# Modulation of a hybrid DiT layer: two of eight weight pieces multiplied whole in fp32, more load buffers, the first latent norms queued behind the modulation's rows

## Chip, core and metric

The kernel runs on one core of one Trainium2 chip. The metric is the device time of one execution in microseconds (us); a smaller number is better. Times before were taken in three runs, and one execution was profiled.

## What is computed

One layer (DEPTH 1) of a diffusion backbone over 2048 latent tokens and 256 context tokens of width 1024, all in float32. It begins with the adaLN modulation, from which everything else takes its input:

```python
def _layer(x, ctx, c, c_ctx, ..., w_mod, b_mod, w_in, ...):
    shift, scale, gate = jnp.split(jax.nn.silu(c) @ w_mod + b_mod, 3, axis=-1)
    shift_c, scale_c, gate_c = jnp.split(jax.nn.silu(c_ctx) @ w_mod + b_mod, 3, axis=-1)
    h = _rmsnorm(x, norm_w) * (1.0 + scale[:, None]) + shift[:, None]
    hc = _rmsnorm(ctx, norm_w) * (1.0 + scale_c) + shift_c
    w_state, w_rest = w_in[:, :N_STATE], w_in[:, N_STATE:]
    ...
```

`w_mod` is 1024 x 3072. The change concerns the first two thirds of it (shift and scale, 1024 x 2048, 8 MB), the two vectors `c` and `c_ctx` that it multiplies, and the order of the first norms. Behind it stand the projections of `h` and `hc` by `w_in`, a bidirectional gated DeltaNet, a windowed attention, their merge and the output projection; the change leaves their code as it is.

## The kernel before

The kernel is written in a tile framework. A scheduler, which works with a model of time of its own, orders the instructions of each engine when the program is built, and the engines then run these queues strictly in order, with semaphores between them. `tc.issue_after(ins)` adds no semaphore: it only makes instructions of the block stand behind `ins` in the queue of the engine on which `ins` runs.

**Splitting.** The TensorE multiplies in `float32r`, one pass at reduced mantissa. To keep fp32 accuracy the kernel splits each operand into a rounded part and the rest: `wmh` is the rounded copy that ScalarE (ACT) writes, `wml` is `wm - wmh`, which VectorE (DVE) writes.

**Modulation (lines 260 to 327).** The rows `c`, `c_ctx`, `norm_w` and `b_mod` are loaded and transposed; `silc` is silu of the two vectors, 128 x 8 x 2, and `sil4` holds its rounded part in columns 0 and 1 and the rest in columns 2 and 3. Then come two halves, `j = 0` (shift) and `j = 1` (scale). Each half goes through eight pieces `k` of `w_mod`, 128 x 1024 (512 KB) each:

- line 303: SyncE (SP) issues the load of the piece into one of seven buffers `wm`
- line 306: ACT rounds it into `wmh`; line 307: DVE writes `wml` (two buffers each)
- line 310: four matmuls of 512 columns add the products of `sil4[:, k]` with both parts into two PSUM tiles `mps` of 4 x 512; the four rows are two vectors by two parts

After the pieces 2 and 3 of the first half the two context blocks are loaded (`load_x`, line 280) and normalized (`norm_x`, lines 289 to 295: a sum of squares half on ACT and half on DVE, a power -0.5 on GpSimd at line 72, one multiplication on DVE).

At the end of a half, line 318 copies the two `mps` into one row tile `mrow`, the first 512 columns on ACT and the others on DVE; `mrow` takes its buffer from those of `wm`. Line 321 turns the rows into columns with eight small fp32 matmuls by `sel`, which also adds the two parts; line 323 adds the bias into `modT`. The first half gives `modB` (line 325), the second `modA` (line 327). `wm_dma` is the last load of a piece; loads that are not to stand ahead of it use `issue_after(wm_dma.ins)`.

**What waits for it.** `make_h` transposes normalized blocks (line 336), applies `modA` and `modB` on ACT (line 337), and splits the result into `hh` (GpSimd, line 339) and `hl` (DVE, line 340). First comes `make_h(pre, ...)` for the two context blocks. `tm_weights` loads the state columns of `w_in` in eight pieces `wr` with three buffers (line 357) and splits them (ACT line 358, DVE line 359). `tm_dense` (lines 366 to 368) multiplies, `state_pair` finishes. The loop `for gi in range(8)` then loads two latent blocks at a time, normalizes them (`norm_x`, line 489), makes their `h` and multiplies. All this is the first stage; the long projections follow.

**Space.** The tiles of the modulation lie in the pool `p0m` at the upper end of the SBUF. When it is closed, the pools `hB2` (`hh3`, `hl3`, 32 KB a partition), `hC` (`hh4`, `hl4`, 16 KB) and `p1a` (among others `wn`, `vst`, `kh`, `ks`, `cw`, some 15 KB) take their place in this order from above, and `p1w` with `wr` lies below them. A tile that overlaps an earlier one waits for the last use of that one alone.

Of the kernel before, what the change touches and what calls it, by code (L numbers as in the profile page):

```python
# [7 lines left out]
F32 = mybir.dt.float32  # L8
F32R = mybir.dt.float32r
# [7 lines left out]
L, LC, D = 2048, 256, 1024  # L17
KT = D // 128
NB, NCB = L // 128, LC // 128
# [9 lines left out]
def f32(ap):  # L29
    return ap.bitcast(F32)  # L30


def hybrid(tc, ins, out, dbg=None, upto=9):
    nc = tc.nc
    V, S, G, T = nc.vector, nc.scalar, nc.gpsimd, nc.tensor
    ctx = ExitStack()
    with ctx:
        _hybrid(ctx, tc, nc, V, S, G, T, ins, out, dbg, upto)


def _hybrid(ctx, tc, nc, V, S, G, T, ins, out, dbg, upto):
# [28 lines left out]
    def rsq(o, x, j=0):  # L70

        G.tensor_tensor(o, x, expo[:, j:j + 1].to_broadcast(list(x.shape)), op=ALU.pow)
# [5 lines left out]
    silc = pers.tile([128, KT, 2], F32, name="silc")  # L78
# [66 lines left out]
    def psum(tag, shape, dt=F32, name=None):  # L145
        _, p, banks = pst["left" if tag in pst["left"][2] else "right"]
        return p.tile(shape, dt, name=name or tag, tag=tag, bufs=banks[tag])
# [104 lines left out]
    if True:  # L252
# [3 lines left out]
        pm = pm_.__enter__()  # L256
# [14 lines left out]
        sil4 = pm.tile([128, KT, 4], F32R, name="sil4")  # L271
        V.tensor_copy(sil4[:, :, 0:2], silc)
        V.tensor_tensor(sil4[:, :, 2:4], silc, f32(sil4[:, :, 0:2]), op=ALU.subtract)
        sel = pm.tile([4, 2], F32, name="sel")
        V.tensor_tensor(sel, ident[0:4, 0:2], ident[0:4, 2:4], op=ALU.add)

        def load_x(c):
            xt = px.tile([128, D], F32, name="xt")
            src = ins["ctx"][0, c * 128:(c + 1) * 128] if c < NCB else ins["x"][0, (c - NCB) * 128:(c - NCB + 1) * 128]
            dma(xt, src)  # L280
            return xt

        def norm_x(c, xt):
            ss = px.tile([128, 2], F32, name="ss")
            for j in range(2):
                junk = px.tile([128, 512], BF16, name="junk", bufs=1)
                xs = xt[:, j * 512:(j + 1) * 512]
                if j == 0:
                    S.activation(junk, xs, AF.Square, scale=D ** -0.5, accum_out=ss[:, j:j + 1])
                else:  # L290
                    junk2 = px.tile([128, 512], BF16, name="junk2", bufs=1)
                    V.scalar_tensor_tensor(junk2, xs, 1.0 / D, xs, op0=ALU.mult, op1=ALU.mult, accum_out=ss[:, j:j + 1])
            V.tensor_scalar(ss[:, 0:1], ss[:, 0:1], ss[:, 1:2], EPS, op0=ALU.add, op1=ALU.add)
            rsq(rstd[:, c:c + 1], ss[:, 0:1])
            V.tensor_scalar(xt, xt, rstd[:, c:c + 1], None, op0=ALU.mult)

        pre = []
        modT = pm.tile([128, 16, 2], F32, name="modT")
        for j in range(2):
            mps = [psum("acc" if n == 0 else "hps", [4, 512], name=f"mps{n}") for n in range(2)]  # L300
            for k in range(KT):
                wm = pm.tile([128, D], F32, name="wm", bufs=7)
                wm_dma = dma(wm, ins["w_mod"][0, k * 128:(k + 1) * 128, j * D:j * D + D])
                wmh = pm.tile([128, D], F32R, name="wmh", bufs=2)
                wml = pm.tile([128, D], F32R, name="wml", bufs=2)
                S.copy(wmh, wm)
                V.tensor_tensor(wml, wm, f32(wmh), op=ALU.subtract)
                for w in (wmh, wml):
                    for n in range(2):
                        T.matmul(mps[n], lhsT=sil4[:, k], rhs=w[:, n * 512:(n + 1) * 512],  # L310
                                 start=k == 0 and w is wmh, stop=k == KT - 1 and w is wml)
                if j == 0 and 2 <= k < 2 + NCB:
                    c = k - 2
                    pre.append(load_x(c))
                    norm_x(c, pre[c])
            mrow = pm.tile([4, D], F32, name="mrow", tag="wm", bufs=7)
            for n in range(2):
                (V.tensor_copy if n % 2 else S.copy)(mrow[:, n * 512:n * 512 + 512], mps[n])
            mtp = psum("kt", [128, 8, 2], name="mtp")
            for i in range(8):  # L320
                T.matmul(mtp[:, i], lhsT=mrow[:, i * 128:i * 128 + 128], rhs=sel, start=True, stop=True)
            mt = modT[:, j * 8:j * 8 + 8]
            V.tensor_tensor(mt, mtp, bm[:, j * 8:j * 8 + 8].unsqueeze(2).to_broadcast([128, 8, 2]), op=ALU.add)
            if j == 0:
                V.tensor_copy(modB, mt)
            else:
                V.scalar_tensor_tensor(modA, mt, 1.0, nw.unsqueeze(2).to_broadcast([128, KT, 2]), op0=ALU.add, op1=ALU.mult)

        def make_h(xts, hi, lo, cc):
            n = len(xts) * 128  # L330
            for k in range(0, KT, 2):
                h32 = px.tile([128, 2, 256], F32, name="h32", bufs=2)
                for i in range(2):
                    ps = psum("hps", [128, 512])
                    for j, xt in enumerate(xts):
                        T.transpose(ps[:, j * 128:(j + 1) * 128], xt[:, (k + i) * 128:(k + i + 1) * 128], ident)
                    S.activation(h32[:, i, :n], ps[:, :n], AF.Identity, scale=modA[:, k + i, cc:cc + 1],
                                 bias=modB[:, k + i, cc:cc + 1])
                G.tensor_scalar(hi[:, k:k + 2], h32[:, :, :n], 1.0, 1.0, op0=ALU.mult, op1=ALU.mult)
                V.tensor_tensor(lo[:, k:k + 2], h32[:, :, :n], f32(hi[:, k:k + 2]), op=ALU.subtract)  # L340
# [21 lines left out]
        def tm_dense(c, wh, wl, n):  # L362
            ps = acc([128, 512], name="tmps")
            xh, xl = hsrc(c)
            for k in range(KT):
                T.matmul(ps[:, :n], lhsT=xh[:, k], rhs=wh[:, k], start=k == 0, stop=False)
                T.matmul(ps[:, :n], lhsT=xl[:, k], rhs=wh[:, k], start=False, stop=False)
                T.matmul(ps[:, :n], lhsT=xh[:, k], rhs=wl[:, k], start=False, stop=k == KT - 1)
            return ps[:, :n]
# [113 lines left out]
        for gi in range(8):  # L483
            xts = []
            for j in range(2):
                c = NCB + gi * 2 + j
                with tc.issue_after(wm_dma.ins):
                    xts.append(load_x(c))
                norm_x(c, xts[j])
            o = gi % 2 * 256  # L490
            make_h(xts, hh[gi // 2][:, :, o:o + 256], hl[gi // 2][:, :, o:o + 256], 0)
            if gi == 7:
                px_.__exit__(None, None, None)
                wq_ = tc.tile_pool(name="wts", bufs=2, reuse_waits="tile")
                wq = wq_.__enter__()
            c = NCB + gi * 2
            state_pair(c, [tm_dense(c + j, wh, wl, NST) for j in range(2)])
# [1088 lines left out]
```

## Time and profile before

| | us |
|---|---|
| median of three runs | 2004.95 |
| lowest and highest of them | 2003.56 and 2009.0 |
| span of the profiled execution | 2004.9 |

| engine | busy us in the span | share |
|---|---|---|
| TensorE, matmul (PE) | 1921.2 | 96% |
| VectorE (DVE) | 1509.2 | 75% |
| ScalarE (ACT) | 807.4 | 40% |
| GpSimd (POOL) | 692.6 | 35% |

The profile has one page and a trace behind it that answers further views: groups of instructions by line, waits, a timeline, and windows. In the timeline a row gives the start, the duration, the engine, the line, the operation, what it writes and reads, how many instructions are merged in it, and in brackets the idle time of the engine before it and what ended that. SPq is the queue of DMA issues: its rows are the times of the issue, not of the data. In the windows a row gives a stretch of the span, the busy time and number of instructions of each engine, the granted TensorE clock (1.00 is full speed), the busy share of the 16 DMA engines and the GB/s that they moved. Busy time of PE counts a matmul from its start to a modelled end, so that matmuls that follow each other overlap.

### The profile page before, as it was taken

Reading aid. Unit: us, or ns where it says so; the run is one execution under the profiler, and the core shown is the slowest. Engines: PE = TensorE matmul, PEld = TensorE weight load, DVE = VectorE, ACT = ScalarE, POOL = GpSimd, SP = SyncE. Lnnn points to the kernel's source line nnn. Section 1 sums busy time; section 2 is a strip of 40 time slices with the busy share of each in tenths; the row PEclk is TensorE's granted clock in tenths of the full one; section 3 lists DMA queues with packets and bytes.
Section 4 is the critical chain, followed back from the end, with each engine's and each line's share of the span. In section 5 each row is a group of like instructions: output and inputs, shape, how many; then the busy total and the mean of one; then the engine's idle time right before and its main releaser. Section 6 shows DMA issues by size and latency. Waiting matters only on the chain. (4 is left out here: it accounts for less than half of the span.)

```text
span 2004.9 us, 32107 instructions
## 1 busy us (share of the span) xinstructions
PE 1921.2 (96%) x10947; PEld 1611.0 (80%) x10947; DVE 1509.2 (75%) x2871; ACT 807.4 (40%) x1998; POOL 692.6 (35%) x768
## 2 busy tenths in 40 slices
PE   6999999989999999999999999999989999999998
PEld 3888888779998778877888888788768888877786
DVE  6979766667776899999777776535587777747888
ACT  5755545554444322111222233224675655532221
POOL 1652210225543202004222233323456444420675
PEclk8999999999999999999999999999999999999999
DMA  7542326764546733537887777755355555456454
GB/s 252 175 127 94 98 87 154 184 162 157 161 143 166 189 113 113 142 90 216 225 255 221 224 213 217 193 176 165 126 187 173 176 162 165 129 165 211 137 169 136
DMA packets 387704, 333.12 MB, mean 166 GB/s; under 512 B 83993, under 2 KB 307537, under 8 KB 386901
## 3 DMA queue, kind: packets, MB, share of 16 engines
q1 hardware_dynamic: 352244, 288.60, 49.9%
q10 hardware_dynamic: 35296, 42.48, 6.0%
q8 instruction: 87, 1.43, 0.3%
q14 instruction: 77, 0.62, 0.1%
HBM read 220.28 MB, written 109.13 MB: 164 GB/s over the span
## 5 line engine op out<-in xcount | busy, mean ns | idle before, releaser
L524 PE MATMUL rps<-hh,wh 128*128 128x512 f32 x768 | 309.6, 403 | 5.0 <-DVE rt L818 3.8
L526 PE MATMUL rps<-hh,wl 128*128 128x512 f32 x768 | 309.0, 403 | 0.0
L525 PE MATMUL rps<-hl,wh 128*128 128x512 f32 x768 | 307.7, 401 | 0.0
L563 DVE SCALAR_TENSOR_TENSOR cacc<-y,cw,cacc 128x512 f32<-128x512 f32 (+1 forms) x224 | 163.2, 750 | 22.9 <-ACT cacc L561 18.9
L524 PEld LDWEIGHTS rps<-hh,wh 128*128 128x128 f32 x768 | 145.7, 190 | 39.8 <-DVE rt L818 4.3
L525 PEld LDWEIGHTS rps<-hl,wh 128*128 128x128 f32 x768 | 145.8, 190 | 32.7
L526 PEld LDWEIGHTS rps<-hh,wl 128*128 128x128 f32 x768 | 145.7, 190 | 32.8
L524 PE MATMUL lps<-hh,wh 128*128 128x512 f32 (+1 forms) x448 | 171.6, 383 | 0.2 <-ACT y L634 0.2
L525 PE MATMUL lps<-hl,wh 128*128 128x512 f32 (+1 forms) x448 | 171.3, 382 | 0.0
L526 PE MATMUL lps<-hh,wl 128*128 128x512 f32 (+1 forms) x448 | 171.2, 382 | 0.0
L945 DVE TENSOR_TENSOR pl<-pt,ph 128x512 fp32r<-128x512 f32 x156 | 105.4, 685 | 41.9 <-ACT ph L943 41.2
L943 ACT CAST ph<-pt 128x512 fp32r<-128x512 f32 x156 | 90.2, 585 | 109.9 <-PE pt L941 76.8
L917 DVE CUSTOM_DVE_ANT_0 pr<-sc,band,sk 128x640 f32<-128x640 f32 (+1 forms) x128 | 106.6, 862 | 34.4 <-PE sc L913 18.3
L816 ACT ACTIVATE rt<-rps 128x512 f32<-128x512 f32 x96 | 57.3, 596 | 181.6 <-PE rps L526 167.8
L749 DVE TENSOR_TENSOR N<-N,btmp 128x62 f32<-128x62 f32 (+30 forms) x124 | 117.2, 945 | 3.0
L747 DVE TENSOR_TENSOR btmp<-N 128x62 f32<-128x62 f32 (+30 forms) x124 | 116.6, 940 | 3.1
L927 POOL TENSOR_SCALAR pr<-pr,sm 128x640 f32<-128x640 f32 (+1 forms) x128 | 99.7, 799 | 55.5 <-DVE sm L925 39.0
L919 ACT ACTIVATE pr<-pr,sm 128x640 f32<-128x640 f32 (+1 forms) x128 | 104.0, 815 | 20.4 <-DVE sm L917 20.4
L246 DVE TENSOR_TENSOR wl<-wr,wh 128x512 fp32r<-128x512 f32 x120 | 92.7, 786 | 24.7 <-POOL wh L245 21.9
L1231 PE MATMUL pps<-yh,wph 128*128 128x512 f32 x256 | 104.8, 411 | 4.3 <-ACT yh L1211 2.2
L245 POOL TENSOR_SCALAR wh<-wr 128x512 fp32r<-128x512 f32 x72 | 48.6, 690 | 170.3 <-PE lps L525 97.2
L1232 PE MATMUL pps<-yl,wph 128*128 128x512 f32 x256 | 100.9, 396 | 0.0
(374 smaller groups left out, 5044.2 us busy)
## 6 DMA issues: line engine op xcount, KB each, us to landing
wr<-in_w_in_dram SPq DMA_DIRECT2D x120, 256.0 KB
kw<-Ksp SPq DMA_DIRECT2D x28, 384.0 KB
x<-vsp SPq DMA_DIRECT2D x36, 256.0 KB
k<-ksp SPq DMA_DIRECT2D x34, 256.0 KB
kT<-kTsp SPq DMA_DIRECT2D x34, 256.0 KB
wm<-in_w_mod_dram SPq DMA_DIRECT2D x16, 512.0 KB
xt<-in_x_dram SPq DMA_DIRECT2D x16, 512.0 KB
dtl<-Dsp SPq DMA_DIRECT2D x32, 256.0 KB
```

The source lines that it names most:

```text
L524: T.matmul(ps, lhsT=wh[:, k], rhs=xh[:, k], start=k == 0, stop=False)
L525: T.matmul(ps, lhsT=wh[:, k], rhs=xl[:, k], start=False, stop=False)
L526: T.matmul(ps, lhsT=wl[:, k], rhs=xh[:, k], start=False, stop=k == kt - 1)
L563: V.scalar_tensor_tensor(a, y[:, t:t + n], cw[:, m, t:t + 1], a, op0=ALU.mult, op1=ALU.add)
L747: V.tensor_tensor(tv, A[:, m + 1:, m].unsqueeze(2).to_broadcast([h1 + n, r, m]), A[:, m, 0:m].unsqueeze(1).to_broadcast([h1 + n, r, m]), o ...
L749: V.tensor_tensor(A[:, m + 1:, 0:m], A[:, m + 1:, 0:m], tv, op=ALU.add)
L917: V.tensor_tensor_reduce(s_, ps[:, o:768], band[:, b0:b0 + W + 256], -0.125, sk[:, 1, hd:hd + 1], ALU.add, ALU.min, sm[:, h, 1:2])
L919: S.activation(s_, s_, AF.Exp, scale=-1.0, bias=sm[:, h, 1:2], accum_out=sm[:, h, 2:3])
L927: G.tensor_scalar(p[:, h, :W + 256], p[:, h, :W + 256], sm[:, h, 3:4], 1.0, op0=ALU.mult, op1=ALU.mult)
L945: V.tensor_tensor(pl, pt, f32(ph), op=ALU.subtract)
L1231: T.matmul(ps, lhsT=wh[:, k, ms], rhs=hs[k], start=k == 0, stop=False)
L1232: T.matmul(ps, lhsT=wh[:, k, ms], rhs=ls[k], start=False, stop=False)
```

## The change

Pieces 3 and 7 of each half are no longer split: they are multiplied as they came, in fp32, by `silz`, which holds `silc` in columns 0 and 1 and zeros in 2 and 3, so that the sum still has four rows. Each of their two matmuls is one `T.matmul` call. The load buffers `wm` (and with them `mrow`) go from seven to nine, `wmh` and `wml` from two to three each. The context blocks are loaded and normalized behind the pieces 4 and 6 in place of 2 and 3. The instructions of `norm_x` for the first two latent blocks (`gi == 0`) stand behind the two copies of the second half's rows (line 318) on ACT and on DVE; their loads are not bound so.

```diff
+        silz = pm.tile([128, KT, 4], F32, name="silz")
+        V.memset(silz, 0.0)
+        V.tensor_copy(silz[:, :, 0:2], silc)
...
+        WHOLE = (3, 7)
...
-                wm = pm.tile([128, D], F32, name="wm", bufs=7)
+                wm = pm.tile([128, D], F32, name="wm", bufs=9)
                 wm_dma = dma(wm, ins["w_mod"][0, k * 128:(k + 1) * 128, j * D:j * D + D])
-                wmh = pm.tile([128, D], F32R, name="wmh", bufs=2)
-                wml = pm.tile([128, D], F32R, name="wml", bufs=2)
+                if k in WHOLE:
+                    for n in range(2):
+                        T.matmul(mps[n], lhsT=silz[:, k], rhs=wm[:, n * 512:(n + 1) * 512], start=False, stop=k == KT - 1)
+                    continue
+                wmh = pm.tile([128, D], F32R, name="wmh", bufs=3)
+                wml = pm.tile([128, D], F32R, name="wml", bufs=3)
...
-                                 start=k == 0 and w is wmh, stop=k == KT - 1 and w is wml)
-                if j == 0 and 2 <= k < 2 + NCB:
-                    c = k - 2
+                                 start=k == 0 and w is wmh, stop=False)
+                if j == 0 and k in (4, 6):
+                    c = k // 2 - 2
                     pre.append(load_x(c))
                     norm_x(c, pre[c])
-            mrow = pm.tile([4, D], F32, name="mrow", tag="wm", bufs=7)
-            for n in range(2):
-                (V.tensor_copy if n % 2 else S.copy)(mrow[:, n * 512:n * 512 + 512], mps[n])
+            mrow = pm.tile([4, D], F32, name="mrow", tag="wm", bufs=9)
+            rows_out = [(V.tensor_copy if n % 2 else S.copy)(mrow[:, n * 512:n * 512 + 512], mps[n]) for n in range(2)]
...
-                norm_x(c, xts[j])
+                with ExitStack() as behind:
+                    if gi == 0:
+                        for r in rows_out:
+                            behind.enter_context(tc.issue_after(r.ins))
+                    norm_x(c, xts[j])
```

## The prediction

> **What bounds the kernel now.** I began with the page. PE is busy in 96% of the span, so time is won only where the PE row is thin, and that is its first digit. The change lies there too.
>
> ```profile
> span 2004.9 us, 32107 instructions
> PE   6999999989999999999999999999989999999998
> ```
>
> The windows show what each engine does there:
>
> ```profile
> 10.00:20.00 10.00, 6.32 (x20) 1.63 (x19) 8.48 (x14) 6.37 (x10) 2.07 (x2) 0.98 1.03 410
> 20.00:30.00 10.00, 9.57 (x40) 4.66 (x39) 6.30 (x8) 4.66 (x6) 0.00 (x0) 0.68 0.77 261
> 26.00:27.00 1.00, 1.00 (x7) 0.86 (x6) 0.96 (x3) 0.00 (x0) 0.00 (x0) 0.71 0.13 12
> 43.00:44.00 1.00, 0.51 (x2) 0.11 (x2) 1.00 (x4) 0.35 (x2) 1.00 (x2) 0.50 0.00 0
> 80.00:90.00 10.00, 8.68 (x69) 8.06 (x69) 9.89 (x29) 8.76 (x26) 7.28 (x9) 1.00 0.67 222
> 180.00:220.00 40.00, 40.00 (x198) 33.07 (x197) 34.41 (x61) 23.90 (x56) 10.00 (x9) 1.00 0.32 96
> ```
>
> From 180 us PE is full (40.00 of 40). Before that, while the latent blocks are made, DVE is nearly full (9.89 of 10) and PE close behind (8.68). Neither has a fixed start: if the work before them ends earlier by some time, they end earlier by it. So the question is when the modulation ends. The loads ran at 410 GB/s at first and at 12 GB/s at 26 us. SP's own waits tell why: its loads stood waiting for buffers, for `wml` to have read them or for the first `mrow` to be done with.
>
> ```profile
> SPq L303 <- DVE wml L307: 12.6, 8, 3.1
> SPq L303 <- PE mtp L321: 3.7, 1, 3.7
> ```
>
> The timeline gives the end of the modulation:
>
> ```profile
> 36.54 0.63 PE L310 MATMUL mps<-wml,sil 128*4 128x512 f32 x2
> 36.97 0.57 ACT L318 COPY mrow<-mps 4x512 f32<-4x512 f32 x1 [0.68 <-PE mps L310]
> 39.68 0.69 DVE L292 SCALAR_TENSOR_TENSOR junk<-xt 128x512 bf16<-128x512 f32 x1 [2.06 <-DMA xt<-in_x_dram]
> 40.30 0.67 DVE L318 COPY mrow<-mps 4x512 f32<-4x512 f32 x1
> 40.30 0.08 DVE L292 DVE_READ_ACCUMULATOR junk<-xt 128x1 f32 x1
> 41.81 0.21 DVE L293 TENSOR_SCALAR ss<-ss 128x1 f32<-128x1 f32 x1
> 41.03 1.86 PE L321 MATMUL mtp<-sel,mrow 4*128 4x2 f32 x8 [2.38 <-DVE mrow L318]
> 43.70 0.16 DVE L327 SCALAR_TENSOR_TENSOR modA<-modT,craw 128x16 f32<-128x16 f32 x1
> 43.90 1.94 ACT L337 ACTIVATE h<-hps,modB,modA 128x256 f32<-128x256 f32 x4 [0.65 <-DVE modA L327]
> ```
>
> The last product ends at 37.17 us (36.54 + 0.63). ACT copies its half at once. DVE's half is copied only at 40.30, although it was ready: in DVE's queue a norm stands ahead of it, and that waited for the load of a latent block until 39.68. The columns, `modA` and the first `h` at 43.90 all follow from this copy.
>
> **The rows behind the norms.** With the norms behind both copies, DVE copies right after the last product. Alone this takes 40.30 back to about 37.3, since DVE was idle then: **3.0 us**. What the norm's edge holds back on DVE and ACT is only the norms. Two of them cost DVE 2 x (0.69 + 0.08 + 0.21) = 2.0 us and fit beside the 1.86 us of line 321, for which DVE waits anyway; if they ran ahead of `modT` and late, they would cost up to 1 us. Their loads are not held.
>
> **Two pieces whole.** The rows for a split piece and for an fp32 matmul:
>
> ```profile
> L307 DVE TENSOR_TENSOR wml<-wm,wmh 128x1024 fp32r<-128x1024 f32 x16 | 19.3, 1223 | 2.9 <-ACT wmh L306 2.6
> L306 ACT CAST wmh<-wm 128x1024 fp32r<-128x1024 f32 x16 | 16.7, 1048 | 8.7 <-DMA wm<-in_w_mod_dram 3.1 <-DVE wml L307 2.0 <-PE hps L336 1.7
> 7.64 1.01 PE L310 MATMUL mps<-wmh,sil 128*4 128x512 f32 x2 [3.33 <-ACT wmh L306]
> 30.41 0.62 PE L310 MATMUL mps<-wml,sil 128*4 128x512 f32 x2
> 30.87 0.61 PE L310 MATMUL mps<-wmh,sil 128*4 128x512 f32 x2
> 21.06 1.05 PE L310 MATMUL mps<-wml,sil 128*4 128x512 f32 x2
> 21.92 1.05 PE L310 MATMUL mps<-wmh,sil 128*4 128x512 f32 x2
> 745.92 1.02 PE L227 MATMUL gsum<-gacc,mats 128*1 128x512 f32 x2
> 746.87 0.50 PE L524 MATMUL rps<-hh,wh 128*128 128x512 f32 x1
> ```
>
> Four pieces fewer on DVE are 4 x 1.22 = 4.9 us and on ACT 4 x 1.05 = 4.2 us. On PE a pair of split products takes 0.46 us (30.41 to 30.87) at full clock and 0.86 (21.06 to 21.92) at half: 0.93 or 1.71 a piece. The kernel has one fp32 matmul of 512 columns, line 227; it is recorded as two instructions, and the next product follows after 0.95 us. Its stationary side has one column and not four, which should not matter, since the split products have four. A whole piece thus costs 2 x 0.95 = 1.9 us, or by the ratio of the clocks an estimated 3.8 at half clock. PE pays 1 us more for each of the four.
>
> **More buffers.** A load of 512 KB at 410 GB/s takes 1.28 us. The first piece is there by 6.55:
>
> ```profile
> 6.55 1.04 ACT L306 CAST wmh<-wm 128x1024 fp32r<-128x1024 f32 x1 [1.75 <-DMA wm<-in_w_mod_dram]
> ```
>
> With nine buffers `mrow` has one of its own, and the last load needs one that piece 7 frees near 20 us. So I take the 18 loads (16 pieces, two context blocks) as unbroken. Piece 7 is the tenth: 6.55 + 9 x 1.28 = 18.1 us. The last: 6.55 + 17 x 1.28 = 28.3.
>
> **The new end of the modulation.** First half: piece 7 lands at 18.1, and its 1.9 us on PE follow directly, where a split piece would pass ACT and DVE first: 20.0. Here the rows stand of the passage between the halves, and the transposes that PE does in it:
>
> ```profile
> 23.55 0.68 DVE L318 COPY mrow<-mps 4x512 f32<-4x512 f32 x1 [1.75 <-PE mps L310]
> 23.94 1.94 PE L321 MATMUL mtp<-sel,mrow 4*128 4x2 f32 x16 [0.43 <-ACT mrow L318]
> 26.28 1.34 PE L336 MATMUL hps<-ident,xt 128*128 128x128 f32 x6
> ```
>
> Second half: copy 0.7, line 321 1.94, transposes 1.34, then 6 x 0.93 + 2 x 1.9 = 9.4 us of products. By then DVE (six pieces of 1.22 since 20 us) and the loads (28.3) are ahead, so PE is the limit: 20.0 + 0.7 + 1.9 + 1.3 + 9.4 = 33.3 at full clock. The granted clock was 0.68 in the mean from 20 to 30 us; if it was full or half, that is 6.4 us at half, and half of these falling into the second half's products would add 1.6: 34.9. Where the transposes or first products fill PE while it waits for the copy, up to 1.5 us go off. Bounds 32 to 36; I take **34.0**, between. The Trainium skill, "TensorE: Matmul & The Clock Gate", Part 1, speaks against the change: an idle TensorE falls to half rate and comes back only after about 3.4 us of sustained work. The passage between the halves would be such an idle time; by the rule the products behind it would end at 35.0 and the kernel at 1999.7, where by the 34.0 above it is 1998.7. The 0.68 agrees with stretches of this kind.
>
> **The sum.** DVE's copy moves from 40.30 to 34.05, 6.25 us. Line 321, the bias and `modA` follow as before, and so does `h`: 43.90 becomes 37.65. To keep it, the state weights must come earlier too:
>
> ```profile
> 27.84 1.37 SPq L357 DMA_DIRECT2D wr<-in_w_in_dram  x3
> 30.68 2.40 SPq L280 DMA_DIRECT2D xt<-in_x_dram  x2
> 36.86 8.37 SPq L357 DMA_DIRECT2D wr<-in_w_in_dram  x5
> 42.12 1.13 ACT L358 CAST wh<-wr 128x272 fp32r<-128x272 f32 x3 [0.39 <-DMA wr<-in_w_in_dram]
> L358 ACT CAST wh<-wr x8: 410/417/418, 35.1 to 47.0; 128x272 fp32r<-128x272 f32 x8
> L337 ACT ACTIVATE h<-hps,modB,modA x72: 548/567/623, 43.9 to 132.3; 128x256 f32<-128x256 f32 x72
> 36.40 1.14 DVE L359 TENSOR_TENSOR wl<-wr,wh 128x272 fp32r<-128x272 f32 x3
> L303 SPq DMA_DIRECT2D wm<-in_w_mod_dram x16: 328/328/646, 2.7 to 27.5; - x16
> ```
>
> They are issued in three and five, with the latent blocks between; the second lot waits until DVE has split the first, from 36.40 on. All stand behind the last piece's load, which leaves SP at some 21 (piece 7's buffer comes free at 20.0) in place of 27.5 us, and DVE has its last `wml` near 30 (the second half's piece 6 lands at 6.55 + 16 x 1.28 = 27.0, then 1.05 + 1.22) in place of 36.4. So they come some 6 us earlier. The last of them was cast at 47.0, 3.1 us behind the first `h`, and eight parts of `h` take ACT 8 x 0.567 = 4.5 us, so this chain had about 1.4 us in hand. `silz` is two small instructions on DVE before the first piece has landed at 6.55; uncovered they would cost about 0.4 us, twice the 0.21 of line 293. The context loads two and three pieces later delay norms whose result PE needs only for transposes: nothing, or the 1 us that is in the bounds. Forecast: 2004.9 - 6.25 = **1998.7 us**. The profiled span and the median of the runs, 2004.95, are the same.
>
> **The rivals.**
>
> *PE takes the place of DVE (slower).* If PE stays at half clock, a half costs 6 x 1.71 + 2 x 3.8 = 17.9 us. In the second half alone: 20.0 + 0.7 + 1.9 + 1.3 + 17.9 = 41.8, the copy then in place of 40.30: 2006.4. In both halves (7.64, where the first product starts, + 17.9 = 25.5): 47.3, 2011.9. It decides from an end of the products at 40.3 us on. For it: 0.50 at 43 us and 0.68 from 20 to 30. Against it: from 10 to 20, with PE busy 6.32 of 10, the clock was 0.98, and the change makes PE busier. 5%, at 2006 to 2012.
>
> *The gain stops at the next load (half of it).* The loads may come later than I let them, by the scheduler's order or because `p0m` grows from 45 to 61 KB a partition and now reaches under `p1a`: the rope tile `cw` then waits for a buffer of `wm`, and SP holds what stands behind it, the second lot of `wr` among it. Then only what the copy gives is kept: 2004.9 - 3.0 = 2001.9. If `cw` waits for the second `mrow`, freed near 37.6, this lot is issued 1 us later than before and nothing is left: 2005. For it: SP waited 3.7 us behind line 321 already. Against it: `cw` can take its turn later, and the chain had 1.4 us in hand. 30% in all: 22% at 2000.5 to 2004, 8% at 2004 to 2006.
>
> *More than forecast.* If PE keeps full clock and fills the gap behind the copy, the products end at 32: 8.2 us, 1996.7; and the stage behind it, at 0.50 where it starts, would win up to 2 us if its half clock ended sooner: 1994.7. 15%.
>
> **How the numbers follow.** The forecast has 50%, from 1996.9 to 2000.5 (ends at 32.2 to 35.8). The range goes from 1995.5 to 2003.5, which leaves out about a tenth on each side. Faster by over 0.3%, about what can be told from no change here, means below 1998.9: somewhat over half of the forecast's 50% and nearly all of the 15%, 0.43; slower by over 0.3% (above 2011) needs the first rival in both halves or a stage behind that is reordered badly, 0.06; the rest, 0.51, lies within.
>
> **What would show it.** In the profile of the changed kernel: DVE's copy of the second rows within 0.2 us of the last product, and that product at 32 to 36 us; records of fp32 matmuls on the whole pieces 0.47 us apart, two for a matmul; no wait of SP's line 303 for line 321; the first `h` near 37.7; the second lot of `wr` cast by 40; and from the first `h` to the end 1961.0 us as before (2004.9 - 43.9). It is wrong if the products end above 37, if `h` waits for PE, SP or `wr` instead, or if those 1961.0 us have another length, which nothing here foresees.

## The result, and the profile after

| | before | after |
|---|---|---|
| median of 20 executions, us | 2002.93 | 1998.24 |
| lowest and highest, us | 1995.94, 2009.0 | 1992.38, 2003.26 |
| span of the profiled execution, us | 2004.9 | 2001.3 |
| ratio after / before, 95% interval | | 0.9976 (0.9967 to 0.9985) |

The changed kernel is faster by 0.24%, that is 4.8 us of 2002.93 (3.0 to 6.6). The forecast was a gain of 6.25 us and 1998.7 us. That 1998.7 and the measured 1998.24 lie so close is in part luck: the forecast took its gain off 2004.9, and the kernel before came out at 2002.93 in twenty executions.

DVE's part of the timeline of the changed kernel, around the modulation's second half:

```profile
21.16 0.68 DVE L325 COPY mrow<-mps 4x512 f32<-4x512 f32 x1 [0.16 <-PE mps L310]
23.03 0.17 DVE L330 TENSOR_TENSOR modT<-mtp,craw 128x16 f32<-128x16 f32 x1 [1.19 <-PE mtp L328]
...
23.32 6.90 DVE L315 TENSOR_TENSOR wml<-wm,wmh 128x1024 fp32r<-128x1024 f32 x6
...
34.03 0.68 DVE L325 COPY mrow<-mps 4x512 f32<-4x512 f32 x1 [2.67 <-PE mps L310]
...
36.16 0.17 DVE L330 TENSOR_TENSOR modT<-mtp,craw 128x16 f32<-128x16 f32 x1
36.24 0.43 DVE L366 TENSOR_TENSOR wl<-wr,wh 128x272 fp32r<-128x272 f32 x1
36.67 0.75 DVE L298 TENSOR_SCALAR xt<-xt,rstd 128x1024 f32<-128x1024 f32 x1
37.34 0.21 DVE L296 TENSOR_SCALAR ss<-ss 128x1 f32<-128x1 f32 x1
37.47 0.17 DVE L334 SCALAR_TENSOR_TENSOR modA<-modT,craw 128x16 f32<-128x16 f32 x1
```

The second copy of the rows starts at 34.03, released by the product that ended at 33.99 (the row of PE below, 32.11 + 1.88). DVE sat idle for 2.67 us before it, so nothing stands in its way. Before, it started at 40.30, 3.1 us after the last product. From `modT` at 36.16 to `modA` at 37.47, however, DVE splits a piece of `wr`, scales a normalized block and does a small step of the next norm, none of which `modA` needs: 1.3 us.

PE from the end of the first half on:

```profile
17.55 0.62 PE L318 MATMUL mps<-wml,sil 128*4 128x512 f32 x2 [0.96 <-DVE wml L315]
...
19.24 1.88 PE L310 MATMUL mps<-wm,silz 128*4 128x512 f32 x4
...
27.43 1.88 PE L310 MATMUL mps<-wm,silz 128*4 128x512 f32 x4
29.24 0.63 PE L318 MATMUL mps<-wmh,sil 128*4 128x512 f32 x2
29.70 0.62 PE L318 MATMUL mps<-wml,sil 128*4 128x512 f32 x2
...
32.11 1.88 PE L310 MATMUL mps<-wm,silz 128*4 128x512 f32 x4
33.92 1.94 PE L328 MATMUL mtp<-sel,mrow 4*128 4x2 f32 x16
```

A whole piece is four records and 1.88 us; a pair of split products stands 0.46 us from the next. ACT's rows and the issues of SP behind it:

```profile
37.67 1.93 ACT L344 ACTIVATE h<-hps,modB,modA 128x256 f32<-128x256 f32 x4 [1.60 <-DVE modA L334]
39.48 0.43 ACT L365 CAST wh<-wr 128x272 fp32r<-128x272 f32 x1
40.67 0.42 ACT L365 CAST wh<-wr 128x272 fp32r<-128x272 f32 x1 [0.76 <-DMA wr<-in_w_in_dram]
```

```profile
37.08 0.42 SPq L388 DMA_DIRECT2D wn<-in_k_norm_w_dram  x1
38.01 0.33 SPq L364 DMA_DIRECT2D wr<-in_w_in_dram  x1
```

The first `h` is at 37.67 and was at 43.90. The last piece of `wr` is issued only at 38.01, behind the small load `wn`, and ACT idles 0.76 us until it has landed.

Three marks of each profile serve below: the end of the modulation's products, the first `h`, and the first long projection (first start of `lps` in the views by tile), which ends the latent stage.

### The profile page after: what moved, and what is told of

Same layout as the page of the kernel before. It is cut to its first block, busy times and chain, and to the rows that moved or that the text cites. A ratio compares the mean times of both kernels' runs of the same rounds, so it can differ in the third digit from the quotient of the medians.

```text
span 2001.3 us, 32092 instructions
## 1 busy us (share of the span) xinstructions
PE 1919.3 (96%) x10947; PEld 1606.1 (80%) x10947; DVE 1508.1 (75%) x2869; ACT 802.4 (40%) x1994; POOL 692.2 (35%) x768
## 5 line engine op out<-in xcount | busy, mean ns | idle before, releaser
L956 DVE TENSOR_TENSOR pl<-pt,ph 128x512 fp32r<-128x512 f32 x156 | 105.4, 686 | 41.9 <-ACT ph L954 41.2
```

Source lines behind the costliest of these rows:

```text
L956: V.tensor_tensor(pl, pt, f32(ph), op=ALU.subtract)
```

## The experiments

Edits are against the changed kernel where nothing else is said. Ratios are to the kernel before, run on the same chip; the kernels themselves stood on several chips. Each rests on 10 to 20 executions of the kernel named, but for "after, again" (4) and "the same, 7 load buffers" (5). "Order" says whether PE, DVE, ACT, POOL and SP issue the same instructions in the same order behind the modulation as the changed kernel does; the kernel before does, but for a few at the start. Stage is from the first `h` to the first `lps`. Marks and spans are of the one profiled execution.

| kernel | ratio (95%) | products end | first `h` | first `lps` | stage | span | order |
|---|---|---|---|---|---|---|---|
| before | 1 | 37.2 | 43.9 | 138.7 | 94.8 | 2004.9 | same |
| before, again | | 36.4 | 41.9 | 137.2 | 95.3 | 2007.0 | same |
| after | 0.9976 (0.9967 to 0.9985) | 34.0 | 37.7 | 134.4 | 96.7 | 2001.3 | same |
| after, again | 0.9957 (0.9940 to 0.9974) | 35.3 | 39.0 | 133.6 | 94.6 | 1994.5 | same |
| rows first alone | 1.0009 (0.9996 to 1.0021) | 35.3 | 42.0 | 137.0 | 95.0 | 2004.5 | other |
| without rows first | 1.0003 (0.9984 to 1.0021) | 34.7 | 38.3 | 141.4 | 103.1 | 2005.4 | other |
| all pieces split | 1.0035 (1.0019 to 1.0052) | 38.0 | 44.5 | 142.2 | 97.7 | 2014.0 | other |
| all split, context late | 1.0004 (0.9988 to 1.0021) | 34.8 | 41.2 | 136.5 | 95.3 | 2006.8 | other |
| piece 7 alone whole | 0.9972 (0.9955 to 0.9989) | 34.0 | 37.6 | 133.9 | 96.3 | 1994.3 | same |
| the same, 7 load buffers | 0.9949 (0.9931 to 0.9966) | 34.0 | 37.7 | 134.0 | 96.3 | 1997.5 | same |
| 7 and 2 buffers | 0.9990 (0.9973 to 1.0007) | 34.8 | 38.8 | 133.9 | 95.1 | 2002.6 | other |
| first columns held | 0.9967 (0.9953 to 0.9981) | 34.1 | 37.7 | 133.1 | 95.4 | 1993.3 | same |
| and norms behind `modA` | 0.9975 (0.9962 to 0.9989) | 32.9 | 35.5 | 129.5 | 94.0 | 1996.4 | other |
| `wr` with five buffers | 0.9994 (0.9974 to 1.0013) | 34.1 | 37.8 | 132.3 | 94.5 | 1996.1 | other |

No kernel here is the one before with piece 7 whole and nothing else, and the move of the context blocks was not tried alone.

**The rows first, alone.** The kernel before with this part only:

```diff
-            for n in range(2):
-                (V.tensor_copy if n % 2 else S.copy)(mrow[:, n * 512:n * 512 + 512], mps[n])
+            rows_out = [(V.tensor_copy if n % 2 else S.copy)(mrow[:, n * 512:n * 512 + 512], mps[n]) for n in range(2)]
...
-                norm_x(c, xts[j])
+                with ExitStack() as behind:
+                    if gi == 0:
+                        for r in rows_out:
+                            behind.enter_context(tc.issue_after(r.ins))
+                    norm_x(c, xts[j])
```

> The kernel before with one part of the change alone: the norms of the first two latent blocks stand behind the two copies of the second half's rows. Seven and two buffers, all pieces split, context blocks behind pieces 2 and 3. Theory A (the copy on DVE was held by a norm that waited for a load, and what is behind follows the first h one to one): the last product stays at 37.2 us, DVE copies at about 37.3 in place of 40.3, first h at 40.9, and the time falls by 3.0 us, 0.15%. Rival (the gain of the change comes from loads and pieces; the copy only hid a wait for something else, such as the state weights or the latent block): first h within 1 us of 43.9, time unchanged.

Measured 1.0009: no gain. DVE in its timeline:

```profile
35.69 0.67 DVE L317 COPY mrow<-mps 4x512 f32<-4x512 f32 x1
38.84 0.69 DVE L292 SCALAR_TENSOR_TENSOR junk<-xt 128x512 bf16<-128x512 f32 x1 [2.48 <-DMA xt<-in_x_dram]
...
40.12 0.69 DVE L292 SCALAR_TENSOR_TENSOR junk<-xt 128x512 bf16<-128x512 f32 x1 [0.26 <-DMA xt<-in_x_dram]
...
40.73 0.17 DVE L322 TENSOR_TENSOR modT<-mtp,craw 128x16 f32<-128x16 f32 x1
```

The copy comes at once, at 35.69. But the two norms now stand behind it and still ahead of `modT`, and they wait for the same loads, issued about as late (29.59 us, before 30.68). The wait moved one place down the queue: `modT` comes at 40.73 and the first `h` at 42.0, between the 41.9 and 43.9 of the kernel before.

**Everything but the rows first.**

```diff
-                with ExitStack() as behind:
-                    if gi == 0:
-                        for r in rows_out:
-                            behind.enter_context(tc.issue_after(r.ins))
-                    norm_x(c, xts[j])
+                norm_x(c, xts[j])
```

> The changed kernel without this one part: whole pieces and more buffers stay, the norms of the first two latent blocks are free again. Theory A taken strictly: a norm stands ahead of DVE's copy again, which then waits for the latent block; first h at 40 to 41 us, 3 us later than the 37.7 of the changed kernel. Rival (the latent blocks are now loaded some 5 us earlier, so a norm in front finds its data and runs in the time in which DVE waits for the products anyway): products end at 34.0 as in the changed kernel, DVE copies within 0.5 us of it, and first h is at 36.4 to 37.7, no later and perhaps earlier, because modA no longer stands behind norms.

Its DVE rows:

```profile
31.96 0.68 DVE L295 SCALAR_TENSOR_TENSOR junk<-xt 128x512 bf16<-128x512 f32 x1
...
34.70 0.68 DVE L325 COPY mrow<-mps 4x512 f32<-4x512 f32 x1 [2.05 <-PE mps L310]
```

The norm stands ahead of the copy again, but finds its block at 31.96, since the blocks are now issued from 26.35 us on. The copy waits for PE alone, and the first `h` is at 38.3, 3.6 us behind the last product; with the norms behind it was 3.7. In the head this part is worth nothing beside the others. And yet no gain is left that can be told from noise: 1.0003 (0.9984 to 1.0021). The stage that follows took 103.1 us in the one profile of this kernel, and the windows show DVE emptier in it and PE as busy with fewer matmuls at a lower clock (the second fence is of the changed kernel):

```profile
78.00:98.00 20.00, 17.23 (x104) 16.22 (x105) 15.88 (x43) 11.77 (x31) 12.24 (x15) 0.74 0.42 125
```

```profile
78.00:98.00 20.00, 17.21 (x133) 15.62 (x131) 19.46 (x49) 13.23 (x38) 13.45 (x17) 1.00 0.52 172
```

In the same 20 us PE does 104 matmuls in place of 133 and DVE 43 operations in place of 49. In the program, what differs there is the order alone: without the edge some 60 of PE's and 50 of DVE's instructions of this stage stand elsewhere. So a single part taken out changes two things, the head and the order behind it. The experiments marked "same" are free of this. That the other order is what makes the stage long isn't shown: the kernel with five `wr` buffers and the one with 7 and 2 buffers have about as many instructions elsewhere, and their stages are 94.5 and 95.1 us. Whether the lower clock follows from the order or came by itself, one profile doesn't say.

**All pieces split.**

```diff
-        WHOLE = (3, 7)
+        WHOLE = ()
...
-                                 start=k == 0 and w is wmh, stop=False)
+                                 start=k == 0 and w is wmh, stop=k == KT - 1 and w is wml)
```

> The changed kernel with no whole piece: all eight are split in each half, nine and three buffers, norms behind the rows. Theory A (with DVE's share of two pieces back, DVE and not PE limits the second half, but only by a little): products end at 34.5 to 35.5 us in place of 34.0, first h 38.2 to 39.2, whole pieces worth about 1 us. Rival (the 4.9 us that they take off DVE count in full for the second half's part, 2.4 us and more): products end at 36.4 or later, first h at 40 or later.

PE around the end of its first half, and the windows of the same execution:

```profile
19.43 0.63 PE L318 MATMUL mps<-wmh,sil 128*4 128x512 f32 x2
22.42 0.78 PE L318 MATMUL mps<-wml,sil 128*4 128x512 f32 x2 [2.37 <-DVE wml L315]
23.48 3.57 PE L328 MATMUL mtp<-sel,mrow 4*128 4x2 f32 x16 [0.28 <-ACT mrow L325]
```

```profile
20.00:22.00 2.00, 0.05 (x1) 0.00 (x0) 1.52 (x2) 0.00 (x0) 0.45 (x1) 1.00 1.05 420
22.00:24.00 2.00, 1.30 (x5) 0.61 (x5) 1.04 (x2) 1.15 (x2) 0.00 (x0) 0.68 1.00 399
24.00:26.00 2.00, 2.00 (x11) 2.00 (x11) 0.00 (x0) 2.00 (x3) 0.00 (x0) 0.50 1.05 418
...
30.00:32.00 2.00, 2.00 (x6) 0.55 (x5) 2.00 (x2) 0.99 (x1) 0.00 (x0) 0.50 0.70 281
```

The last piece must pass ACT and DVE, where a context norm stands ahead of it, and PE waits 2.37 us for it. Behind this pause the granted clock is 0.50 until about 32 us, and line 328 takes 3.57 us and not 1.94. The products end at 38.0, the first `h` is at 44.5, and the kernel is slower than before: 1.0035. The order behind differs too, so how much of the time the head alone costs isn't known.

**All split, the context blocks behind the pieces 6 and 7**, so that no norm stands ahead of the last piece's split:

```diff
-        WHOLE = (3, 7)
+        WHOLE = ()
...
-                if j == 0 and k in (4, 6):
-                    c = k // 2 - 2
+                if j == 0 and k in (6, 7):
+                    c = (6, 7).index(k)
```

> No whole piece, nine and three buffers, norms behind the rows, and the context blocks behind the pieces 6 and 7; the order behind the modulation differs in some 60 places on TensorE and 70 on VectorE. Theory A (the whole last piece is what saves PE from waiting for ACT and DVE at the end of each half, where a wait can cost the full clock): products end at 35 to 38.5 us, first h at 39 to 44; the time is then 1.5 to 6 us above the changed kernel. Rival (what made the kernel without whole pieces slow was only the order of the stages behind it): products end at 34 to 35, and the time is within 1.5 us of the changed kernel.

The products end at 34.8, nearly as early as with whole pieces, though at half clock from 21 to 27 us:

```profile
21.00:27.00 6.00, 5.68 (x26) 4.99 (x25) 4.62 (x8) 4.23 (x5) 0.56 (x1) 0.50 1.02 409
```

The first half ends where it does in the changed kernel: DVE copies its rows at 21.15 and there at 21.16. So in these two profiles the end of the products owes only 0.8 us to the whole pieces, once no norm stands ahead of the last split; this end fits the rival. But `modA` comes only at 40.24 and the first `h` at 41.2. DVE has its last `wml` at 34.1 in place of 30.2, its splits of `wr` come later by as much, SP issues the second lot of `wr` from 34.49 on (30.60 in the changed kernel), and `modT` and `modA` stand among the splits that wait for it; ACT even casts the last piece, at 40.90, ahead of the first `h`. That mark fits theory A. The ratio is 1.0004.

**Piece 7 alone whole.**

```diff
-        WHOLE = (3, 7)
+        WHOLE = (7,)
```

> The changed kernel with only the last piece of each half whole; piece 3 is split. The order of the instructions is that of the changed kernel on every engine, but for the piece itself, so that the stages behind can be compared. Theory A (at full clock the second half is shared between DVE and PE): 1.15 us more on DVE, 1 us less on PE in each half; products end 0 to 1.2 us later than the 34.0 of the changed kernel, first h at 37.7 to 38.9, time 0 to 1.2 us longer. Rival (splitting lets PE idle so long that its clock falls to half, as with no whole piece, where the products ended at 38.1): products end at 36 or later, first h at 40 or later, time 2 us and more longer.

Same order, same end. The rows of DVE and of PE:

```profile
23.42 8.03 DVE L315 TENSOR_TENSOR wml<-wm,wmh 128x1024 fp32r<-128x1024 f32 x7
...
33.99 0.68 DVE L325 COPY mrow<-mps 4x512 f32<-4x512 f32 x1 [1.40 <-PE mps L310]
```

```profile
32.07 1.88 PE L310 MATMUL mps<-wm,silz 128*4 128x512 f32 x4
```

DVE has one more `wml` (8.03 us for seven in place of 6.90 for six) and PE 1 us less; they cancel. The copy is at 33.99 in place of 34.03 and the first `h` at 37.6 in place of 37.7. In the head, piece 3 whole is worth nothing.

**The same with seven load buffers in place of nine** (three of `wmh` and `wml` stay):

```diff
-        WHOLE = (3, 7)
+        WHOLE = (7,)
...
-                wm = pm.tile([128, D], F32, name="wm", bufs=9)
+                wm = pm.tile([128, D], F32, name="wm", bufs=7)
...
-            mrow = pm.tile([4, D], F32, name="mrow", tag="wm", bufs=9)
+            mrow = pm.tile([4, D], F32, name="mrow", tag="wm", bufs=7)
```

> The changed kernel with seven load buffers in place of nine, three each for the split parts; the same order of instructions on every engine. Theory A (unbroken loads move the second half): SP's loads wait for buffers again, the last piece's load leaves SP some 3 to 6 us later than the 21.1 us of the changed kernel, products end 0.5 to 2 us later than 34.0, first h at 38.2 to 39.7. Rival (PE is the limit and the loads have that much in hand): products end within 0.3 us of 34.0, first h within 0.5 of 37.7, the same time.

SP's waits in it, and those of the changed kernel in the second fence:

```profile
SPq L307 <- DVE wml L315: 6.6, 5, 2.1
SPq L307 <- PE mps L310: 5.3, 2, 3.2
```

```profile
SPq L307 <- PE mps L310: 4.3, 2, 2.3
SPq L307 <- DVE wml L315: 2.2, 2, 1.5
```

SP waits 11.9 us for these buffers in place of 6.5, and the modulation ends where it did (34.0 and 37.7). The loads had that much in hand, and two of the nine buffers are worth nothing in the head. The ratio, 0.9949, is the lowest of all, but the changed kernel on the same chip gave 0.9957.

**Seven and two buffers**, the sizes of before, with both pieces whole:

```diff
-                wm = pm.tile([128, D], F32, name="wm", bufs=9)
+                wm = pm.tile([128, D], F32, name="wm", bufs=7)
...
-                wmh = pm.tile([128, D], F32R, name="wmh", bufs=3)
-                wml = pm.tile([128, D], F32R, name="wml", bufs=3)
+                wmh = pm.tile([128, D], F32R, name="wmh", bufs=2)
+                wml = pm.tile([128, D], F32R, name="wml", bufs=2)
```

> The changed kernel with the seven and two buffers of before: whole pieces and the norms behind the rows stay. Theory A (the buffers keep the loads unbroken, which is what moves the second half): SP's loads wait for the first half's mrow again, products end at 35.5 to 37, first h at 39 to 40.5. Rival (the whole pieces alone free the engines, and the loads were early enough): products end at 34.0 to 34.5, first h at 37.7 to 38.2.

The products end 0.8 us later (34.8) and the first `h` 1.1 us (38.8). The first row is ACT's last `wmh`, the second DVE's last `wml`:

```profile
30.02 1.05 ACT L314 CAST wmh<-wm 128x1024 fp32r<-128x1024 f32 x1 [1.96 <-PE mps L318]
31.10 1.23 DVE L315 TENSOR_TENSOR wml<-wm,wmh 128x1024 fp32r<-128x1024 f32 x1 [1.78 <-ACT wmh L314]
```

ACT's last cast waits for PE to be done with an earlier `wmh`; with three of them it ran at 27.03, when its load had landed. So the third buffer for the split parts counts here, not the loads. The ratio is 0.9990, with another order behind; how much of it comes from the head and how much from the order isn't known.

**Two tries to do better.** In the changed kernel DVE stands idle for 1.19 us before `modT` of the first half, and the second half's `wml` wait behind it. The first kernel (piece 7 alone whole) puts `modT` and `modB` of the first half behind the second half's second `wml`; the next also holds DVE's part of the norms until `modA`.

```diff
-        WHOLE = (3, 7)
+        WHOLE = (7,)
...
-                V.tensor_tensor(wml, wm, f32(wmh), op=ALU.subtract)
+                wml_out = V.tensor_tensor(wml, wm, f32(wmh), op=ALU.subtract)
+                if (j, k) == (1, 1):
+                    with tc.issue_after(wml_out.ins):
+                        V.tensor_tensor(held[0], held[1], bm[:, 0:8].unsqueeze(2).to_broadcast([128, 8, 2]), op=ALU.add)
+                        V.tensor_copy(modB, held[0])
...
+            if j == 0:
+                held = (mt, mtp)
+                continue
             V.tensor_tensor(mt, mtp, bm[:, j * 8:j * 8 + 8].unsqueeze(2).to_broadcast([128, 8, 2]), op=ALU.add)
-            if j == 0:
-                V.tensor_copy(modB, mt)
-            else:
+            if j == 1:
```

> The changed kernel with only piece 7 whole and with the first half's bias (modT, modB) behind the second half's first two wml on DVE; the order of all instructions behind the modulation is that of the changed kernel. Theory A (in the second half DVE stood idle for 1.2 us before the bias, and with one whole piece DVE sets the pace): DVE begins the second half's wml at 21.9 in place of 23.3 us, products end at 32.2 to 33.2 in place of 34.0, first h at 36 to 37, time 0.5 to 1.5 us below the changed kernel. Rival (PE, with its rows turned first until 23, is the limit): products end within 0.3 us of 34.0.

```diff
-                V.scalar_tensor_tensor(modA, mt, 1.0, nw.unsqueeze(2).to_broadcast([128, KT, 2]), op0=ALU.add, op1=ALU.mult)
+                modA_out = V.scalar_tensor_tensor(modA, mt, 1.0, nw.unsqueeze(2).to_broadcast([128, KT, 2]), op0=ALU.add, op1=ALU.mult)
...
-                        for r in rows_out:
+                        for r in (rows_out[0], modA_out):
```

> The kernel one_held with the norms of the first two latent blocks behind modA on DVE, in place of behind DVE's copy. In the changed kernel 1.3 us of other work lies between modT and modA. Theory A: first h another 0.9 us earlier than in one_held. The order of the latent blocks' stage differs here from the changed kernel's in some places (about 50 on TensorE, 45 on VectorE). Theory A (a head that is earlier moves all): time 1 us below one_held. Rival (the order of that stage weighs more than the head): the stage from the first h to the first long projection, 94.6 to 96.7 us in the changed kernel, is longer by 2 us and more, and the time is not below one_held's.

The second half became shorter, as meant: from the first copy to the end of the products 22.54 to 34.06 us = 11.5, where the changed kernel took 21.16 to 33.99 = 12.8. In the first kernel's profile its copy was later, because the clock was low before it:

```profile
18.00:20.00 2.00, 2.00 (x6) 0.41 (x4) 1.49 (x4) 0.00 (x0) 0.32 (x1) 0.50 1.03 410
```

In the second one it was not, and with the norms behind `modA` the first `h` came at 35.5, 2.2 us ahead of the changed kernel's. But its time, 0.9975, is that of the changed kernel, and the first kernel's, 0.9967, cannot be told from it either.

**Five buffers for `wr`**, so that the last of them need not wait for a split:

```diff
-                wr = pw.tile([128, NST], F32, name="wr", tag="wr", bufs=3)
+                wr = pw.tile([128, NST], F32, name="wr", tag="wr", bufs=5)
```

> The changed kernel with five buffers in place of three for the pieces of the state weights, and nothing else. The scheduler then puts the instructions behind the modulation in another order (some 260 places on TensorE, 190 on VectorE). Theory A (the time follows the first h): the state weights land earlier, first h at 37.7 or up to 1 us earlier, time the same as or up to 1 us below the changed kernel. Rival (what the scheduler makes of the order behind weighs as much as the whole change): first h as said, but the stage up to the first long projection differs by 3 us and more from 94.6 to 96.7 us, and the time by as much from the changed kernel's.

The head is the same (37.8), the order another, the stage 94.5 us. Here all pieces of `wr` are cast before the first `h`, which comes no earlier for it, so the late `wr` did not hold the first `h` of the changed kernel. What it cost behind stays open: the ratio, 0.9994, is no better, and its interval overlaps that of 0.9976.

**Both kernels once more**, unchanged, for a second profile of each.

> The kernel before, unchanged, for a second profile. Theory A (in the first stretches the granted clock changes between half and full at times that differ from run to run, and the marks of one profile therefore carry an error of some us): last product at 35 to 38 us in place of 37.2, first h at 42 to 44, with half-clock stretches elsewhere than from 20 to 23 and 27 to 29.5 us. Rival (the marks are as fixed as the order of the instructions): each within 0.3 us of the first profile.

> The changed kernel, unchanged, for a second profile and more timed runs. Theory A: first h within 0.5 us of 37.7 where PE keeps full clock from 13 us to the end of the products, up to 2 us later where a half-clock stretch falls in; from the first h to the end 1960 to 1965 us; time 0.15 to 0.3% below before. Rival (the 2.6 us that the first profile has more behind the first h than before belong to the change): they are there again, 1963.5 to 1965.

Before, the first `h` came at 43.9 and at 41.9; after, at 37.7 and at 39.0. From the first `h` to the end the repeat of the changed kernel leaves 1994.5 - 39.0 = 1955.5 us, below what either theory said. The views by tile of the two repeats:

```profile
L337 ACT ACTIVATE h<-hps,modB,modA x72: 546/565/620, 41.9 to 130.7; 128x256 f32<-128x256 f32 x72
```

```profile
L344 ACT ACTIVATE h<-hps,modB,modA x72: 549/566/623, 39.0 to 127.2; 128x256 f32<-128x256 f32 x72
```

## Why the prediction was right, and where its working was not

**The new end of the modulation: the marks as predicted, 34.0 by luck.** 34.0 for the products, 34.05 for the copy and 37.65 for the first `h` were predicted; 33.99, 34.03 and 37.67 came. The whole piece cost 1.88 us (1.9 predicted). But the sum has the first half's products end at 20.0, and they ended at 21.12 (19.24 + 1.88): piece 7 did not follow its load but stood behind the products of the split pieces, for which PE waited 0.96 us on DVE, and DVE had a context norm ahead of them from 13.90 to 16.36. The prediction put these norms at nothing or at the 1 us in its bounds. The second half then took 12.9 us, where the sum has 13.3 at full clock. No load of a piece waited for line 328 (the 321 of before). The last cast of the second lot of `wr` started at 40.67 (by 40 predicted) and delayed nothing that shows in the first `h`. The repeat ended 1.3 us later, at 35.3, inside the bounds.

**The size: the mark of before was one sample, and a late one.** The sum took 40.30 and 43.90 from one execution, and 6.25 us off them. The clock is low in stretches of some 3 us at different places in each execution of the same kernel, and these marks moved with it. Two samples each: before (43.9 + 41.9) / 2 = 42.9, after (37.7 + 39.0) / 2 = 38.35, a difference of 4.55 us, beside 4.8 measured (3.0 to 6.6); the repeat gave a ratio of 0.9957, which is 8.6 us of 2005.6 (5.2 to 12.0). The prediction's 6.25 lies inside the first interval, so that it was too large isn't shown; with a mark of 42.9 the sum would have given 43.90 - 42.9 = 1.0 us less. Two samples carry no more than that, and whether some of the earlier start was lost behind stays open: from the first `h` to the end the spans leave 1961.0 and 1965.1 us before, 1963.6 and 1955.5 after. That these are a constant 1961.0 was a test that the prediction set, and by its own sign it failed there: they are not constant. They differ by 4 to 8 us between executions of one kernel, as much as the effect, and the forecast counted on the difference of single marks to carry through.

**The rows behind the norms: the step that failed.** "Alone this takes 40.30 back to about 37.3 ... 3.0 us" did not hold: alone it gained nothing (1.0009), because the norms wait for their load ahead of `modT` where they had waited ahead of the copy. The prediction allowed this place at most 1 us, the norms' own time; it left out that a norm which waits for a load brings its wait along. In the whole change the sum hid the mistake, since earlier loads ended the wait, and then the edge was worth nothing in the head. DVE's other work between `modT` and `modA`, 1.3 us, was of the size allowed.

**PE as the limit of the second half: half right.** Until about 27 us PE went at the pace of DVE's `wml`, which started only at 23.32 behind `modT`; from there on PE was full. The two errors of the sum, a late first half with DVE's late start behind it, and a clock that stayed full where part of it was taken at half, cancelled to 34.0. In the passage between the halves PE did not go to half clock in this execution (1.00 from 20 to 30 us), so the 35.0 of the prediction, for which it shows no working, did not arise. Nor was the passage much of an idle time: in the prediction's own row PE is busy 9.57 of the 10 us. In the kernel with all pieces split, where PE paused 2.37 us, the clock did go to 0.50 behind the pause.

**More buffers: the loads were not the cause.** Two of the nine load buffers are worth nothing in the head; the third one for the split parts is worth 0.8 us there. The head needs the last piece whole, because DVE is then done earlier with the pieces and free for `wr` and the norms (at 31.5 with piece 7 alone whole, at 34.1 with none and the context late): with none whole the first `h` was at 44.5 and 41.2, with piece 7 alone at 37.6. What of this the clock did was not separated from the work saved (see the last section). Piece 3 could have stayed split in both halves.

**The rivals.** PE in DVE's place: not seen in the changed kernel; the nearest is the kernel with everything split, by a pause and not by PE's own load. The gain stopping at the next load: its event came, `wn` held SP until 37.08 and the last `wr` behind it, but with no cost that shows.

**What it did not foresee** is that the order of the next hundred us depends on every part of the change. That the changed kernel has the order of before was luck that the prediction took for granted. The five ratios of kernels with this order, the repeat among them, lie from 0.9949 to 0.9976; of the seven with another order, only one (0.9975) is as low, though in four of these seven the first `h` comes by 38.8. Where they lose it isn't shown, and some of the intervals overlap: the stage is long without the edge on the norms (103.1 us) and with all pieces split (97.7), but at most 95.3 us in the other five, as before.

## What to carry to other kernels

An instruction that waits for a load, moved down its queue, takes its wait along: look at what it now stands ahead of, and whether the load could be issued earlier instead. Where a pipeline of three engines ends, let the last piece skip the engines that the next stage waits for; one piece of each half was enough here. And before a small gain is read from one profile, profile the same kernel twice: marks in the head moved by 1 to 2 us here, and spans by 2 to 7. An edit that makes the scheduler reorder what stands behind it is no test of the edit alone; compare the order first.

## What was not expected of the hardware

The low clock comes at other times in each execution of the same kernel. In the windows the kernel before has 0.50 from 20 to 23 us in its first profile, and in the second this stretch is full and the low one is earlier:

```profile
20.00:23.00 3.00, 3.00 (x8) 0.87 (x7) 1.78 (x2) 0.54 (x1) 0.00 (x0) 0.50 0.98 382
```

```profile
15.00:18.00 3.00, 2.65 (x6) 0.56 (x7) 2.44 (x6) 2.24 (x3) 1.49 (x1) 0.51 1.02 407
20.00:23.00 3.00, 2.37 (x9) 0.43 (x7) 2.25 (x3) 1.26 (x3) 0.00 (x0) 1.00 1.02 366
```

The Trainium skill, "TensorE: Matmul & The Clock Gate", Part 1, says that the window by which the clock is set runs freely, so that the count of slow matmuls differs from run to run; these rows agree.

But not all of it is chance. The mean granted clock from 12 to 34 us, before and after:

```profile
12.00:34.00 22.00, 17.49 (x68) 6.57 (x65) 16.45 (x22) 13.37 (x15) 2.07 (x2) 0.84 0.86 308
```

```profile
12.00:34.00 22.00, 20.51 (x78) 6.26 (x76) 15.62 (x24) 12.99 (x20) 1.14 (x2) 1.00 0.98 371
```

In the five profiles of kernels without a whole piece it is 0.77 to 0.92 (both of before 0.84), in the nine with one 0.92 or 1.00. An estimate from this: 0.16 x 22 = 3.5 us of full clock, beside the 3.2 us by which the products end earlier. So keeping PE supplied may have gained as much through the clock as through the work saved; no run here separates the two. Over the whole span the clock is 0.984 in both profiles of before, 0.989 and 0.990 in those of the changed kernel. The times mostly go with it within one kernel too: of 35 executions of the kernel before on one chip, one took 1995.59 us at a mean clock of 0.991 and another 2006.79 at 0.985; an estimate of what 0.006 of the clock is worth, 0.006 x 2000 = 12 us, has the size of that difference.

The recorded clock also seems to miss a slow stretch. In the changed kernel it reads 1.00 from 8 to 10 us, where two pairs of products start 0.86 us apart, as the prediction's rows show at 0.50; at full clock it is 0.46.

```profile
8.00:10.00 2.00, 1.75 (x5) 0.34 (x4) 1.98 (x2) 1.75 (x2) 0.00 (x0) 1.00 1.04 424
```

```profile
9.65 1.05 PE L318 MATMUL mps<-wmh,sil 128*4 128x512 f32 x2
10.51 1.05 PE L318 MATMUL mps<-wml,sil 128*4 128x512 f32 x2
```
